# Delta-rule layer: a forward substitution is divided by columns between GpSimd and VectorE, and the query norms move behind GpSimd's share

## The chip, the cores and the metric

The kernel runs on one NeuronCore of a Trainium2 chip. The metric is device time in microseconds (us) of one execution. A core has five engines with a queue each, and each works through its queue in order: TensorE (PE: matmuls and transposes; its weight loads are listed as PEld), VectorE (DVE), ScalarE (ACT), GpSimd (POOL) and SyncE (SP, which here only issues DMAs). Engines wait for each other through semaphores. Before the change the kernel takes 860.06 us (median of 3 runs, 859.24 to 860.62).

## The reference: what is computed

Four residual layers over 256 tokens of width 1024: a pooling mixer, a gated delta-rule layer, an attention layer and the pooling mixer again, all in float32. The change lies in the second, the delta-rule layer. Its core, cut to what matters:

```python
diff = g[..., :, None] - g[..., None, :]
decay = jnp.exp(jnp.where(causal, diff, -jnp.inf))
L = jnp.where(strict, jnp.einsum('bhnid,bhnjd->bhnij', k_beta, k) * decay, 0.0)
A = jnp.eye(C, dtype=L.dtype) + L
sol = lax.linalg.triangular_solve(A, rhs, left_side=True, lower=True)
u_ps, w_cd = sol[..., :dv], sol[..., dv:]
attn = jnp.where(causal, jnp.einsum('bhnid,bhnjd->bhnij', q, k) * decay, 0.0)
...
q = l2norm(q.reshape(B, S, GDN_HEADS, GDN_DK).astype(f32)) * (GDN_DK ** -0.5)
```

There are 8 heads. A unit lower triangular system has to be solved for each head and chunk, and queries and keys are normalised.

## The kernel before

**Precision and weights.** Every large product is three float32r matmuls: a weight tile `raw` is split into `whi` (rounded, ScalarE, L117) and `wlo` (the rest, L119: a subtraction of two tiles in SBUF, on VectorE, or on GpSimd for the k-tiles that the argument `pool` lists). Weights come by SP's queue into three `raw` buffers of two k-tiles each; the split halves sit in rings of nine. So a matmul waits for a `wlo`, a `wlo` for a `whi`, a `whi` for a DMA and for a ring place that a matmul gives back.

**Order.** The program is written in the order of the string `g0 k0 d a0 g1 k1 a1 s q0 v0 i v1 v2 q1 g2 u0 v3 u1 g3` (L559), and a list scheduler (`schedule_with_timeline_sim`, L1242) then sets the order on every engine from its own estimates of time; `tc.issue_after`, wrapped as `later` (L85), holds a step back behind an instruction. That order is fixed when the kernel is built. A projection (`g`, `k`, `q`, `v` and a number) has 8 k-tiles of weights. `k`, `q` and `v` take 96 matmuls of 128x256 each (L127 to L129), then a causal convolution: four ScalarE starts (L633) and 12 VectorE steps (L636), which free the PSUM banks; then a SiLU, and PE transposes (L675 for q and k, L778 for v).

**The substitution.** The chunk here is 128 tokens, so there are 2 x 8 systems of 128x128. Step `a` (L708) writes L transposed to `LT`. Step `s` (L712) inverts the four 32x32 diagonal blocks of each system, 64 blocks in all, one block in a partition: 8 DMAs carry the blocks to DRAM (`d_l`), one brings them back as `Lb` (64 x 32 x 32), and `Tb` starts as 64 unit matrices. Then come 31 rounds r of two GpSimd instructions: an outer product `pr` (L726) of column r of `Lb` below the diagonal and row r of `Tb`, and its subtraction from the rows of `Tb` below r (L730). A round works on 31-r rows and r+1 columns, and each instruction reads what the one before it wrote. `Tb` goes to DRAM (`d_t`, L732) and back in 8 DMAs to the diagonal blocks of `T` (L736). Step `i` (L787) builds the full inverse from `T`: first 16 short matmuls for each of two token tiles (L806) and VectorE's transposes of `T` into `U` (L797), then the rest.

**The query norms.** `queries` (L747) ends with five GpSimd instructions for each half of the heads (L754 to L760): the decay times the queries, and the inverse norm by a power function (`power`, L656). In `values` (L765) GpSimd does the `wlo` of k-tiles 1, 3, 5, 7 of v0 and of 3 and 7 of v1; in `gate` (L551) those of 3 and 7 of g2 and 7 of g3.

Of the kernel before, what the change touches and what calls it, by code (L numbers as in the profile page):

```python
# [13 lines left out]
ALU = mybir.AluOpType  # L14
AX = mybir.AxisListType

P = 128
# [7 lines left out]
EPS = 1e-6  # L25
# [17 lines left out]
def trunk(ctx: ExitStack, tc: tile.TileContext, x, positions, norm_g, pool_w_in, pool_w_grp,  # L43
          pool_scale, pool_w_out, gdn_w_in, gdn_conv, gdn_a_log, gdn_dt_bias, gdn_norm_g,
          gdn_w_out, mla_w_in, mla_q_norm_g, mla_w_uq, mla_kv_norm_g, mla_w_ukv, mla_w_out,
          final_g, out, depth=4, final=True):
    nc = tc.nc
# [22 lines left out]
    def big(name, *dims, dt=F32):  # L70
        return s4.tile([P, *dims], dt, tag="s4", name=name)
# [7 lines left out]
    def small(name, *dims, bufs=2):  # L79
        return sm.tile([P, *dims], F32, tag=name, name=name, bufs=bufs)  # L80
# [4 lines left out]
    def later(*instructions):  # L85

        order = ExitStack()
        for ins in instructions:
            order.enter_context(tc.issue_after(ins))
        return order  # L90


    mark = {}
# [94 lines left out]
    def units(n):  # L188
        return [(k, KU) for k in range(0, n, KU)]
# [141 lines left out]
    def cols_of(w, c0, cols=CW):  # L331
        v = w.rearrange("(k p) c -> p k c", p=P)
        return lambda k0, n: v[:, k0:k0 + n, c0:c0 + cols]
# [201 lines left out]
    def gdn_layer(i, j, hT):  # L535
        H = GDN_H
        M = NT * H
        DV = 256
# [33 lines left out]
        for t in range(NT):  # L572
# [8 lines left out]
                                in1=dtb[:, None, :].to_broadcast([P, NT, H]))  # L581
# [13 lines left out]
                                in1=alog[:, None, :].to_broadcast([P, NT, H]))  # L595
# [14 lines left out]
        for t in range(NT):  # L610
            nc.gpsimd.dma_start(
                out=Gb[t].rearrange("p h s -> p (h s)"),
# [28 lines left out]
        Q, B = 4, 32  # L641
        Tb = big("Tb", B, B)[:M * Q]
# [6 lines left out]
        kT, qT = [], []  # L649
        ktok = big("ktok", H, P)  # L650
        ssq = small("ssq", 2, NT, H, bufs=1)
# [4 lines left out]
        def power(o, a):  # L656
            nc.gpsimd.tensor_tensor(out=o, in0=a, in1=half, op=ALU.pow)
# [25 lines left out]
        def against(dst, rhs, sf, hf, t):  # L683

            ps = bank(aux, "aux").rearrange("p (b s) -> p b s", b=4)
            tt = slice(t * P, (t + 1) * P)
            for b in range(4):
                nc.tensor.matmul(ps[:, b], lhsT=kT[hf][:, b, tt], rhs=rhs[hf][:, b, tt],  # L688
                                 start=True, stop=True)
            for b in range(4):  # L690
                h = 4 * hf + b
                nc.vector.scalar_tensor_tensor(
                    out=dst[t][:, h, :], in0=ps[:, b], scalar=sf[:, t, h:h + 1],
                    in1=DT[t][:, h, :], op0=ALU.mult, op1=ALU.mult)
# [17 lines left out]
        def substitution():  # L712

            d_l = dram.tile([M * Q, B * B], F32, name="d_l")
            lv = d_l.rearrange("(t m d) (r c) -> t d r m c", t=NT, d=Q, r=B)
            for t in range(NT):
                for d in range(Q):
                    nc.sync.dma_start(out=lv[t, d],
                                      in_=LT[t][d * B:(d + 1) * B, :, d * B:(d + 1) * B])
            Lb = big("Lb", B, B)[:M * Q]  # L720
            nc.sync.dma_start(out=Lb, in_=d_l.rearrange("m (r c) -> m r c", r=B))
            pr = small("pr", 256, bufs=1)[:M * Q]
            for r in range(B - 1):
                n, c = B - 1 - r, r + 1
                pv = pr[:, :n * c].rearrange("m (a b) -> m a b", a=n)
                nc.gpsimd.tensor_tensor(out=pv, op=ALU.mult,  # L726
                                        in0=Lb[:, r, r + 1:, None].to_broadcast([M * Q, n, c]),
                                        in1=Tb[:, r:r + 1, :c].to_broadcast([M * Q, n, c]))
                tv = Tb[:, r + 1:, :c]
                nc.gpsimd.tensor_tensor(out=tv, in0=tv, in1=pv, op=ALU.subtract)  # L730
            d_t = dram.tile([M * Q, B * B], F32, name="d_t")
            nc.sync.dma_start(out=d_t.rearrange("m (r c) -> m r c", r=B), in_=Tb)  # L732
            tv = d_t.rearrange("(t m d) (r c) -> t d r m c", t=NT, d=Q, r=B)
            for t in range(NT):
                for d in range(Q):
                    nc.sync.dma_start(out=T[t][d * B:(d + 1) * B, :, d * B:(d + 1) * B],  # L736
                                      in_=tv[t, d])
            nc.vector.reciprocal(rki, rk)
            nc.vector.tensor_tensor(out=kds, in0=rk[:, 0, :], in1=DT[0][:, :, P - 1],
                                    op=ALU.mult)  # L740
            nc.vector.tensor_scalar(neG, eG[:, 1, :], -1.0, None, ALU.mult)
            nc.gpsimd.tensor_tensor(out=ktok, in0=ktok, op=ALU.mult,
                                    in1=kds[:, :, None].to_broadcast([P, H, P]))
# [3 lines left out]
        def queries(hf):  # L747
            if hf == 0:
                at_.extend(big("attnT", H, P) for _ in range(NT))
            channels(qT, 0, hf, 1)  # L750
            for t in range(NT):
                against(at_, qT, rk, hf, t)
            ev = Eb[:, 4 * hf:4 * hf + 4, :]
            nc.gpsimd.tensor_tensor(out=ev, in0=ev, in1=qT[hf][:, :, P:], op=ALU.mult)  # L754
            rh, qh = rq[:, :, 4 * hf:4 * hf + 4], rq2[:, :, 4 * hf:4 * hf + 4]
            nc.gpsimd.tensor_scalar(qh, ssq[:, 1, :, 4 * hf:4 * hf + 4], float(P), EPS * P,
                                    ALU.mult, ALU.add)
            power(rh, qh)
            nc.gpsimd.tensor_tensor(out=qh, in0=rh, in1=rh, op=ALU.mult)
            nc.gpsimd.tensor_scalar(qh, qh, 1.0 / DV, None, ALU.mult)  # L760


        vR = []

        def values(vi):  # L765
            banks = project(cols_of(w_in, 2 * GDN_QK + vi * CW), units(KD), hT, chan=True,
                            pool=((1, 3, 5, 7), (3, 7), (), ())[vi])
            vR.append(big("vR", NT, CW))
            for b in range(2):
                h = 2 * vi + b  # L770
                vc = worka("vc", 2 * S)
                conv(*[(banks[b][:, c * S:(c + 1) * S], 16 + 2 * h + c, vc[:, c * S:(c + 1) * S])
                       for c in range(2)])
                nc.scalar.activation(vc, vc, AF.Silu)
                ps = bank(tps, "tp").rearrange("p (t s) -> p t s", t=NT)
                for t in range(NT):
                    for c in range(2):
                        nc.tensor.transpose(ps[:, t, c * P:(c + 1) * P],  # L778
                                            vc[:, c * S + t * P:c * S + (t + 1) * P], ident)
                for t in range(NT):  # L780
                    nc.scalar.activation(vR[vi][:, t, b * DV:(b + 1) * DV], ps[:, t], AF.Copy,
                                         scale=rki[:, t, h:h + 1])
# [470 lines left out]
```

## Time and profile before

| what | value |
|---|---|
| median of 3 runs | 860.06 us |
| the profiled execution: its time | 859.14 us |
| its span, first to last instruction | 857.4 us |
| around the span (difference) | 1.7 us |
| PE busy | 835.0 us (97%) |
| VectorE, ScalarE, GpSimd busy | 591.2, 488.2, 155.7 us |
| delta-rule layer, roughly | 178 us to 427 us of the span |
| the 31 rounds on GpSimd | 259.8 us to 310.1 us |

In the rows that follow, times are microseconds from the span's start unless marked ns; a timeline row gives start, duration, engine, source line, operation, output and inputs, the shape and how many instructions it merges, and in brackets the engine's idle time before it with what ended that. The table of windows gives the busy time of each engine in a stretch and, as PEclk, the TensorE clock that was granted (1.00 is full).

### The profile page before, as it was taken

How to read it: one execution, taken by the hardware profiler on the slowest of the kernel's cores; microseconds unless marked ns; L12 is line 12 of the kernel's file. 1: busy time of each engine (PE TensorE's matmuls, PEld its weight loads, DVE VectorE, ACT ScalarE, POOL GpSimd, SP SyncE). 2: the span in 40 equal slices, each digit the busy share in tenths (PEclk: the TensorE clock that was granted, in tenths of full speed). 3: DMA queues.
4: the chain of work that ended last, by engine and by line, in shares of the span. 5: the costliest groups of instructions: out<-in, count | busy, mean ns of one | idle time of the engine just before them, and what ended most of it. 6: DMA issues, size and time to landing. Idle time of an engine off the chain costs nothing.

```text
span 857.4 us, 16137 instructions
## 1 busy us (share of the span) xinstructions
PE 835.0 (97%) x5967; PEld 778.7 (91%) x5967; DVE 591.2 (69%) x1138; ACT 488.2 (57%) x1007; POOL 155.7 (18%) x292
## 2 busy tenths in 40 slices
PE   7999999999999969999999999999999999999996
PEld 6999998988999959888979998999989989999986
DVE  4589776456989665656577659778767668866852
ACT  5565555467857435555565654566555476555542
POOL 4000000233248941022212002000000210000012
PEclk9999999999999989999999999999999999999999
DMA  6765556546555462222547676743652547565551
GB/s 199 249 188 188 178 189 213 180 148 206 188 160 176 134 168 102 75 74 99 173 147 215 201 165 172 196 132 95 171 167 79 173 149 218 175 192 183 187 200 50
DMA packets 111288, 140.43 MB, mean 164 GB/s; under 512 B 23340, under 2 KB 53224, under 8 KB 111208
## 3 DMA queue, kind: packets, MB, share of 16 engines
q1 hardware_dynamic: 109056, 138.17, 53.1%
q8 instruction: 47, 0.77, 0.4%
q0 software_dynamic: 320, 1.06, 0.3%
q10 hardware_dynamic: 1832, 0.16, 0.2%
q14 instruction: 33, 0.27, 0.1%
HBM read 137.79 MB, written 1.58 MB: 163 GB/s over the span
## 4 chain that ended last, share of the span: by engine, by line
PE 85%; POOL 7%; DVE 2%; DMA 2%; issue 2%; ACT 1%; SPq 1%; POOLq 0%; ACTq 0%; DVEq 0%
PE acc L167 34%; PE acc L127 12%; PE acc L128 12%; PE acc L129 12%; POOL Tb L730 2%; POOL pr L726 2%; PE aux L127 2%; PE aux L128 2%; PE aux L129 2%; DVE h L303 1%; DMA gain<-in_norm_g_dram 1%; PE aux L688 1%; ACT junk L209 1%; PE aux L806 1%; PE tp L1165 1%
## 5 line engine op out<-in xcount | busy, mean ns | idle before, releaser
L119 DVE TENSOR_TENSOR wlo<-raw,whi 128x512 fp32r<-128x512 f32 (+1 forms) x491 | 338.6, 712 | 163.2 <-ACT whi L117 160.9
L117 ACT CAST whi<-raw 128x512 fp32r<-128x512 f32 (+1 forms) x508 | 301.4, 617 | 261.8 <-PE acc L167 89.8
L127 PE MATMUL acc<-hTh,whi 128*128 128x256 f32 x832 | 235.3, 283 | 1.0 <-DVE cv L636 1.0
L128 PE MATMUL acc<-hTl,whi 128*128 128x256 f32 x832 | 235.8, 283 | 0.0
L129 PE MATMUL acc<-hTh,wlo 128*128 128x256 f32 x832 | 234.7, 282 | 0.0
L127 PEld LDWEIGHTS acc<-hTh,whi 128*128 128x128 f32 x832 | 157.7, 190 | 1.8 <-issue 1.4
L128 PEld LDWEIGHTS acc<-hTl,whi 128*128 128x128 f32 x832 | 157.6, 189 | 0.4
L129 PEld LDWEIGHTS acc<-hTh,wlo 128*128 128x128 f32 x832 | 157.5, 189 | 0.2
L167 PE MATMUL acc<-wlo,yTh 128*128 128x256 f32 (+1 forms) x384 | 116.2, 319 | 0.0
L167 PE MATMUL acc<-whi,yTh 128*128 128x256 f32 (+1 forms) x384 | 116.2, 323 | 0.0
L167 PE MATMUL acc<-whi,yTl 128*128 128x256 f32 (+1 forms) x384 | 92.4, 321 | 0.0
L167 PEld LDWEIGHTS acc<-wlo,yTh 128*128 128x128 f32 x384 | 72.0, 188 | 5.0
L167 PEld LDWEIGHTS acc<-whi,yTh 128*128 128x128 f32 x384 | 71.9, 188 | 5.2
L167 PEld LDWEIGHTS acc<-whi,yTl 128*128 128x128 f32 x384 | 63.1, 188 | 5.6
L291 POOL TENSOR_TENSOR hg<-x,gain 128x256 f32<-128x256 f32 x18 | 14.8, 832 | 259.1 <-DVE x L353 257.4
L167 PE MATMUL acc<-wlo,hTh 128*128 128x512 f32 (+1 forms) x144 | 55.9, 394 | 0.4 <-DVE wlo L119 0.2
L167 PE MATMUL acc<-whi,hTh 128*128 128x512 f32 (+1 forms) x144 | 55.5, 393 | 0.7 <-ACT hTh L195 0.7
L167 PE MATMUL acc<-whi,hTl 128*128 128x512 f32 (+1 forms) x144 | 45.4, 388 | 0.0
L119 POOL TENSOR_TENSOR wlo<-raw,whi 128x512 fp32r<-128x512 f32 x17 | 23.1, 1360 | 70.2 <-ACT whi L117 70.2
L434 POOL COPY win<-u 128x4 f32<-128x4 f32 x8 | 2.8, 354 | 177.0 <-ACT u L428 177.0
L167 PEld LDWEIGHTS acc<-wlo,hTh 128*128 128x128 f32 x144 | 27.3, 190 | 6.8 <-DVE wlo L119 1.7
L167 PEld LDWEIGHTS acc<-whi,hTh 128*128 128x128 f32 x144 | 27.3, 190 | 6.8 <-ACT hTh L195 1.7
(337 smaller groups left out, 1443.3 us busy)
## 6 DMA issues: line engine op xcount, KB each, us to landing
raw<-in_pool_w_in_dram SPq DMA_DIRECT2D x60, 512.0 KB, 4.4
raw<-in_gdn_w_in_dram SPq DMA_DIRECT2D x48, 512.0 KB, 3.9
raw<-in_pool_w_out_dram SPq DMA_DIRECT2D x32, 512.0 KB, 3.7
raw<-in_mla_w_in_dram SPq DMA_DIRECT2D x24, 512.0 KB, 4.4
raw<-in_mla_w_uq_dram SPq DMA_DIRECT2D x36, 256.0 KB, 3.8
raw<-in_pool_w_grp_dram SPq DMA_DIRECT2D x16, 512.0 KB, 4.2
raw<-in_gdn_w_out_dram SPq DMA_DIRECT2D x16, 512.0 KB, 3.5
raw<-in_mla_w_ukv_dram SPq DMA_DIRECT2D x32, 256.0 KB, 3.4
```

What stands on the lines that cost most here:

```text
L117: a = nc.scalar.copy(hi, v)
L119: b = e.tensor_tensor(out=lo, in0=v, in1=hi.bitcast(F32), op=ALU.subtract)
L127: nc.tensor.matmul(o, lhsT=lhs[0], rhs=rhs[0], start=start, stop=False)
L128: nc.tensor.matmul(o, lhsT=lhs[0], rhs=rhs[1], start=False, stop=False)
L129: nc.tensor.matmul(o, lhsT=lhs[1], rhs=rhs[0], start=False, stop=stop)
L167: nc.tensor.matmul(o, lhsT=act(k, t * P, P)[x], rhs=parts[j][z][:, sl], start=k == first and x == z == 0, stop=k == last and x == 1)
L209: nc.scalar.activation(junk[:, :n], src, AF.Square, scale=scale, accum_out=o)
L291: nc.gpsimd.tensor_tensor(out=self.early[t, a], in0=xs[t][:, sl], in1=self.g[:, sl], op=ALU.mult)
L303: nc.vector.scalar_tensor_tensor(out=h[:, cut:], in0=xs[t][:, sl], scalar=r[:, 0:1], in1=self.g[:, sl], op0=ALU.mult, op1=ALU.mult)
L688: nc.tensor.matmul(ps[:, b], lhsT=kT[hf][:, b, tt], rhs=rhs[hf][:, b, tt], start=True, stop=True)
L726: nc.gpsimd.tensor_tensor(out=pv, op=ALU.mult, in0=Lb[:, r, r + 1:, None].to_broadcast([M * Q, n, c]), in1=Tb[:, r:r + 1, :c].to_broadcast ...
L730: nc.gpsimd.tensor_tensor(out=tv, in0=tv, in1=pv, op=ALU.subtract)
```

## The change

The 31 rounds become two independent runs, since a column of the inverse depends on no other column. GpSimd solves columns 0 to 5 in 31 rounds of at most six columns (temporary `prp`). VectorE solves columns 6 to 31 in the 25 rounds from 6 on, which have 31-r rows and r-5 columns (temporary `prv`): 50 instructions. The five query-norm instructions may be issued on GpSimd only after its last subtraction (`mark["blocks"]`), for both halves. And the two `wlo` of v1 that GpSimd did go to VectorE. The program's DMAs are the same in number and size.

```diff
--- before.py
+++ after.py
@@ -719,15 +719,19 @@
                                       in_=LT[t][d * B:(d + 1) * B, :, d * B:(d + 1) * B])
             Lb = big("Lb", B, B)[:M * Q]
             nc.sync.dma_start(out=Lb, in_=d_l.rearrange("m (r c) -> m r c", r=B))
-            pr = small("pr", 256, bufs=1)[:M * Q]
-            for r in range(B - 1):
-                n, c = B - 1 - r, r + 1
-                pv = pr[:, :n * c].rearrange("m (a b) -> m a b", a=n)
-                nc.gpsimd.tensor_tensor(out=pv, op=ALU.mult,
-                                        in0=Lb[:, r, r + 1:, None].to_broadcast([M * Q, n, c]),
-                                        in1=Tb[:, r:r + 1, :c].to_broadcast([M * Q, n, c]))
-                tv = Tb[:, r + 1:, :c]
-                nc.gpsimd.tensor_tensor(out=tv, in0=tv, in1=pv, op=ALU.subtract)
+
+            for e, name, c0, c1 in ((nc.gpsimd, "prp", 0, 6), (nc.vector, "prv", 6, B)):
+                tmp = small(name, 200, bufs=1)[:M * Q]
+                for r in range(c0, B - 1):
+                    n, c = B - 1 - r, min(r + 1, c1) - c0
+                    pv = tmp[:, :n * c].rearrange("m (a b) -> m a b", a=n)
+                    e.tensor_tensor(out=pv, op=ALU.mult,
+                                    in0=Lb[:, r, r + 1:, None].to_broadcast([M * Q, n, c]),
+                                    in1=Tb[:, r:r + 1, c0:c0 + c].to_broadcast([M * Q, n, c]))
+                    tv = Tb[:, r + 1:, c0:c0 + c]
+                    end = e.tensor_tensor(out=tv, in0=tv, in1=pv, op=ALU.subtract)
+                if e is nc.gpsimd:
+                    mark["blocks"] = end.ins
             d_t = dram.tile([M * Q, B * B], F32, name="d_t")
             nc.sync.dma_start(out=d_t.rearrange("m (r c) -> m r c", r=B), in_=Tb)
             tv = d_t.rearrange("(t m d) (r c) -> t d r m c", t=NT, d=Q, r=B)
@@ -751,20 +755,22 @@
             for t in range(NT):
                 against(at_, qT, rk, hf, t)
             ev = Eb[:, 4 * hf:4 * hf + 4, :]
-            nc.gpsimd.tensor_tensor(out=ev, in0=ev, in1=qT[hf][:, :, P:], op=ALU.mult)
             rh, qh = rq[:, :, 4 * hf:4 * hf + 4], rq2[:, :, 4 * hf:4 * hf + 4]
-            nc.gpsimd.tensor_scalar(qh, ssq[:, 1, :, 4 * hf:4 * hf + 4], float(P), EPS * P,
-                                    ALU.mult, ALU.add)
-            power(rh, qh)
-            nc.gpsimd.tensor_tensor(out=qh, in0=rh, in1=rh, op=ALU.mult)
-            nc.gpsimd.tensor_scalar(qh, qh, 1.0 / DV, None, ALU.mult)
+
+            with later(mark["blocks"]):
+                nc.gpsimd.tensor_tensor(out=ev, in0=ev, in1=qT[hf][:, :, P:], op=ALU.mult)
+                nc.gpsimd.tensor_scalar(qh, ssq[:, 1, :, 4 * hf:4 * hf + 4], float(P), EPS * P,
+                                        ALU.mult, ALU.add)
+                power(rh, qh)
+                nc.gpsimd.tensor_tensor(out=qh, in0=rh, in1=rh, op=ALU.mult)
+                nc.gpsimd.tensor_scalar(qh, qh, 1.0 / DV, None, ALU.mult)
 
 
         vR = []
 
         def values(vi):
             banks = project(cols_of(w_in, 2 * GDN_QK + vi * CW), units(KD), hT, chan=True,
-                            pool=((1, 3, 5, 7), (3, 7), (), ())[vi])
+                            pool=((1, 3, 5, 7), (), (), ())[vi])
             vR.append(big("vR", NT, CW))
             for b in range(2):
                 h = 2 * vi + b
```

The scheduler answers with another order on every engine, in the stretch from q0 to u1 above all. Line numbers from L735 on are larger by 4 to 6 in the changed kernel (L732 there is the subtraction, L784 the transpose of v, L812 the first matmul on `T`).

VectorE, where `Lb` has landed. `Tb` and `prv`, `pr` are the substitution's; `attnT` and `ssq` belong to q0, `vc_3467` and `vc_3484` (before), `vc_3518` and `vc_3535` (after) are the two convolved halves of v0. Before:

```order
L119 TENSOR_TENSOR wlo_3822<-raw_3820,whi_3823 128x512
L679 TENSOR_REDUCE ssq_2522<-sq_3294 128x2x2
L692 SCALAR_TENSOR_TENSOR attnT_3124<-aux_3305,rk_2523,DT_2496 128x128 x4
L679 TENSOR_REDUCE ssq_2522<-sq_3302 128x2x2
L692 SCALAR_TENSOR_TENSOR attnT_3125<-aux_3314,rk_2523,DT_2497 128x128 x4
L636 SCALAR_TENSOR_TENSOR vc_3467<-acc_3328,tap_648,vc_3467 128x255
L636 SCALAR_TENSOR_TENSOR vc_3484<-acc_3329,tap_648,vc_3484 128x255
L119 TENSOR_TENSOR wlo_3826<-raw_3820,whi_3827 128x512
```

Now, at the same place:

```order
L119 TENSOR_TENSOR wlo_3839<-raw_3837,whi_3840 128x512
L728 TENSOR_TENSOR prv_3110<-Lb_3045,Tb_2514 64x25
L732 TENSOR_TENSOR Tb_2514<-Tb_2514,prv_3110 64x25
L728 TENSOR_TENSOR prv_3110<-Lb_3045,Tb_2514 64x48
L732 TENSOR_TENSOR Tb_2514<-Tb_2514,prv_3110 64x24x2
L728 TENSOR_TENSOR prv_3110<-Lb_3045,Tb_2514 64x69
L679 TENSOR_REDUCE ssq_2522<-sq_3345 128x2x2
L732 TENSOR_TENSOR Tb_2514<-Tb_2514,prv_3110 64x23x3
L728 TENSOR_TENSOR prv_3110<-Lb_3045,Tb_2514 64x88
L692 SCALAR_TENSOR_TENSOR attnT_3175<-aux_3356,rk_2523,DT_2496 128x128
L732 TENSOR_TENSOR Tb_2514<-Tb_2514,prv_3110 64x22x4
```

The rounds now stand between VectorE's other work, from here to four `wlo` before its transposes of `T`; between the first and the last of them stand 26 `wlo`, all 36 convolution steps of v0, v1 and v2, and 6 of q1.

PE, at the transposes of v0 (`tp`), between matmuls of v2 (`acc_3784`, `acc_3785` before, `acc_3835`, `acc_3836` after). Before:

```order
L129 MATMUL acc_3785<-hTh1_2267,wlo_3856 128x256
L778 MATMUL tp_3477<-ident_101,vc_3467 128x128 x4
L127 MATMUL acc_3785<-hTh1_2267,whi_3857 128x256
L128 MATMUL acc_3785<-hTl1_2268,whi_3857 128x256
L129 MATMUL acc_3785<-hTh1_2267,wlo_3856 128x256
L127 MATMUL acc_3784<-hTh1_2267,whi_3861 128x256
L128 MATMUL acc_3784<-hTl1_2268,whi_3861 128x256
L129 MATMUL acc_3784<-hTh1_2267,wlo_3860 128x256
L127 MATMUL acc_3784<-hTh1_2267,whi_3861 128x256
L128 MATMUL acc_3784<-hTl1_2268,whi_3861 128x256
L129 MATMUL acc_3784<-hTh1_2267,wlo_3860 128x256
L778 MATMUL tp_3494<-ident_101,vc_3484 128x128 x4
```

Now:

```order
L127 MATMUL acc_3835<-hTh0_2258,whi_3878 128x256
L128 MATMUL acc_3835<-hTl0_2259,whi_3878 128x256
L129 MATMUL acc_3835<-hTh0_2258,wlo_3877 128x256
L784 MATMUL tp_3528<-ident_101,vc_3518 128x128 x4
L784 MATMUL tp_3545<-ident_101,vc_3535 128x128 x4
L127 MATMUL acc_3836<-hTh0_2258,whi_3840 128x256
L128 MATMUL acc_3836<-hTl0_2259,whi_3840 128x256
L129 MATMUL acc_3836<-hTh0_2258,wlo_3839 128x256
```

Both groups of transposes stand together now, 95 matmuls behind the products of q0's keys and queries (L688), where the first stood 125 and the second 134 matmuls behind them. From those products to the first matmul on `T` there are 299 matmuls of 128x256 and 48 of 128x512 before, and 302 and 48 now.

## The prediction

> **What bounds the kernel now.** I read the waits of PE over the delta-rule layer first, then the chain of work that ended last, PE's timeline, and the table of windows. PE is busy for 97% of the span, and of its waits in this layer one is long: the first matmul on `T` waits for the DMA that brings `T` back.
>
> ```profile
> PE 835.0 (97%) x5967; PEld 778.7 (91%) x5967; DVE 591.2 (69%) x1138; ACT 488.2 (57%) x1007; POOL 155.7 (18%) x292
> ```
>
> ```profile
> PE aux L806 <- DMA T<-d_t: 7.4, 1, 7.4
> PE acc L127 <- DVE cv L636: 1.0, 1, 1.0
> ```
>
> ```profile
> 310.12 2.94 DMA d_t<-Tb
> 313.98 2.02 DMA T<-d_t
> ```
>
> ```profile
> 259.78 0.23 POOL L726 TENSOR_TENSOR pr<-Lb,Tb 64x31 f32<-64x31 f32 x1 [1.25 <-DMA Lb<-d_l]
> 309.85 0.24 POOL L730 TENSOR_TENSOR Tb<-Tb,pr 64x31 f32<-64x31 f32 x1
> ```
>
> ```profile
> 308.45 0.28 PE L129 MATMUL acc<-hTh,wlo 128*128 128x256 f32 x1
> 316.09 3.65 PE L806 MATMUL aux<-T,LT 128*128 128x64 f32 x16 [7.36 <-DMA T<-d_t]
> 320.07 0.42 PE L129 MATMUL acc<-hTh,wlo 128*128 128x256 f32 x1
> 326.57 1.89 PE L806 MATMUL aux<-T,LT 128*128 128x64 f32 x16
> ```
>
> GpSimd's rounds run from 259.78 to 310.09; 6.0 us later, at 316.09, PE has `T`. It had finished what it had at 308.73 and so idles 7.36 us. Then it runs at half clock:
>
> ```profile
> 265.00:275.00 10.00, 10.00 (x87) 10.00 (x87) 10.00 (x20) 6.54 (x14) 9.45 (x14) 1.00 0.56 161
> 315.00:325.00 10.00, 8.91 (x45) 8.94 (x46) 4.88 (x6) 4.50 (x11) 0.00 (x0) 0.54 0.61 179
> 325.00:335.00 10.00, 10.00 (x99) 9.84 (x99) 6.35 (x12) 6.18 (x14) 1.69 (x2) 1.00 0.20 58
> ```
>
> The sixteen matmuls of L806 take 3.65 us there and 1.89 at full clock (1.8 lost), and the 15 of 128x256 that follow it by 324.6 come 0.21 us apart instead of 0.118 (1.4 lost); with eight slowed transposes (estimate 0.6) the half clock costs 3.8 us. With the 1.0 us wait for `cv` the stretch loses 7.4 + 3.8 + 1.0 = 12 us: that is all that an earlier `T` could save. In the window from 265 to 275 (columns: PE, PEld, DVE, ACT, POOL busy) VectorE is as full as PE: 10.00 of 10.00 us.
>
> **The change part by part.** *GpSimd's share.* A round's instruction has (31-r) rows by at most six columns: 2 x 2,531 = 5,062 elements in 62 instructions, against 10,912 before.
>
> ```profile
> 260.44 0.28 POOL L726 TENSOR_TENSOR pr<-Lb,Tb 64x60 f32<-64x60 f32 x1
> 264.62 0.46 POOL L726 TENSOR_TENSOR pr<-Lb,Tb 64x156 f32<-64x156 f32 x1
> ```
>
> From 0.28 us for 60 elements to 0.46 for 156 is 1.9 ns an element and 0.17 us fixed; with the gap of 0.08 between instructions 62 x 0.25 + 5,062 x 0.0019 = 25 us. The old rounds took 50.3 us, 6.3 of them other instructions in between; by the same formula they would be 36, so some 8 us were contention. GpSimd will end between 285 and 295, long before it is needed. Behind it stand the query norms and the first half's product, now 4 us of GpSimd (1.27 and 1.67 the longest), and then two `wlo` of g2, which PE needs after 300: no cost. The norms held back are first read here:
>
> ```profile
> 366.43 0.20 POOL L900 TENSOR_TENSOR oss<-oss,rq 128x2 f32<-128x2 f32 x1 [21.93 <-ACT junk L209]
> ```
>
> That is 70 us later, and GpSimd idles 22 us before it, so this part costs nothing either.
>
> *VectorE's share* is the term that decides. It has 2 x 2,925 = 5,850 elements in 50 instructions, none of which the trace has on VectorE. The nearest rows:
>
> ```profile
> 196.90 0.17 DVE L589 TENSOR_SCALAR beta<-beta 128x16 f32<-128x16 f32 x1 [0.71 <-ACT beta L585]
> 197.01 0.17 DVE L587 TENSOR_SCALAR e<-e 128x16 f32<-128x16 f32 x1
> 199.26 0.17 DVE L593 TENSOR_SCALAR sp<-sp 128x16 f32<-128x16 f32 x1
> 199.46 0.17 DVE L594 TENSOR_TENSOR lga<-sp,alog 128x16 f32<-128x16 f32 x1
> 244.08 0.15 DVE L703 TENSOR_TENSOR s<-rk,beta 128x8 f32<-128x8 f32 x1
> ```
>
> ```profile
> L119 DVE TENSOR_TENSOR wlo<-raw,whi 128x512 fp32r<-128x512 f32 x11 | 7.2, 687 | 5.5 <-ACT whi L117 5.5
> ```
>
> Independent small instructions start 0.11 us apart, dependent ones (L594 reads what L593 wrote) 0.20: about 0.09 and 0.18 fixed. From 0.15 us at 8 elements to 0.687 at 512 it is 1.07 ns an element. In the changed order 16 of the 50 stand right behind the one that they read: 16 x 0.18 + 34 x 0.09 + 5,850 x 0.00107 = 12.2 us. The rest of what VectorE does from the first of them to the last:
>
> ```profile
> 287.21 2.03 DVE L636 SCALAR_TENSOR_TENSOR vc<-acc,tap,vc 128x254 f32<-128x254 f32 x5
> 355.84 2.16 DVE L692 SCALAR_TENSOR_TENSOR attnT<-aux,rk,DT 128x128 f32<-128x128 f32 x8 [0.41 <-PE aux L688]
> 259.61 0.67 DVE L679 TENSOR_REDUCE ssq<-sq 128x4 f32<-128x512 f32 x1
> ```
>
> 42 convolution steps at 0.39 (16.4), 26 `wlo` at 0.60 start to start (15.6), 8 `attnT` at 0.27 (2.2), two sums at 0.60 (1.2): 35.4 us. Together 47.6 us, so from 259.8 VectorE ends its columns at 307.4 at the earliest. `Lb` may land half a microsecond sooner, as a weight load now stands behind the `d_l` DMAs and not among them on SP's queue; I leave that out. SP's other DMAs keep their places. The wait of the first one for `Lb` holds up q0's sums and `attnT` behind it; the first of these started at 259.61, so by 0.2 us.
>
> *Contention between the two shares* has no row of its own and needs bounds. Below: nothing. Above, these rows:
>
> ```profile
> 244.49 1.90 POOL L742 TENSOR_TENSOR ktok<-ktok,kds 128x1024 f32<-128x1024 f32 x1 [0.89 <-DVE kds L739]
> 245.11 1.30 DVE L705 TENSOR_TENSOR s<-s,rk 128x8 f32<-128x8 f32 x1
> ```
>
> ```profile
> L119 DVE TENSOR_TENSOR wlo<-raw,whi 128x512 fp32r<-128x512 f32 x20 | 16.9, 851 | 0.6 <-ACT whi L117 0.6
> ```
>
> L705 has the form of L703 and takes 1.30 us instead of 0.15: it ends with GpSimd's `ktok`, at 246.4. So an instruction of VectorE with two SBUF inputs can be held until GpSimd's is done. `wlo`, `prv` and the subtraction are all of this kind; the convolution reads PSUM. If VectorE had to stand aside for all of GpSimd's 25.5 us (20 in the rounds without gaps, 5.5 in the four long ones behind them), and 42% of that fell on VectorE's other work (19.8 of 47.6 us), it would lose 0.58 x 25.5 = 15 us. Between the ends I go by the group of 20 `wlo` measured beside the busy rounds, from 259.6 to 292.7: 851 ns against 687, so 0.16 us each. About 15 `wlo` and 30 of the new instructions fall into GpSimd's time: 45 x 0.16 = 7.2, and 1.3 for the long instructions behind: 8.5 us. VectorE ends at 315.9, `T` is there at 321.9.
>
> The Trainium skill (SBUF — State Buffer, section "Who interferes with whom") says that a VectorE instruction with two SBUF inputs and a GpSimd instruction that reads SBUF share a port under an exclusive lock, held for the whole instruction. L705's 1.30 us agrees; the 851 ns of the `wlo`, beside a GpSimd that was busy nearly all the time, show mild blocking. By the rule at its strictest the sum would take the upper bound, which is a rival below.
>
> *PE's order.* Now, 95 matmuls behind q0's products, PE comes to both groups of v0's transposes. At 0.118 us each from 258.96 this is 270.2.
>
> ```profile
> 258.96 0.37 PE L128 MATMUL acc<-hTl,whi 128*128 128x256 f32 x1
> 272.92 0.63 ACT L774 ACTIVATE vc<-vc 128x512 f32<-128x512 f32 x1
> 273.83 0.60 PE L778 MATMUL tp<-ident,vc 128*128 128x128 f32 x4
> ```
>
> Before, the first group came at 273.83, when its SiLU was just ready. Now VectorE must first have done 13 of the new instructions (2.7 us), the sums and `attnT` (3.4), 8 `wlo` (4.8) and 15 convolution steps (5.9): 16.8 us, or 20 with 0.16 for each of 21; from 259.8 that is 279.8, and with the SiLU 280.4. PE, which holds weights enough, stands still from 270.2 for 10 us (at least 6.9), and queued behind it is all the rest of v2, q1 and g2. After so long a wait I count half clock again, 3.8 us. Its remaining work to the first matmul on `T` is 207 matmuls (24.4), 48 of 0.233 (11.2, by the rows below) and 16 transposes (estimate 1.4, from the four in 0.60):
>
> ```profile
> 291.55 0.40 PE L167 MATMUL acc<-whi,hTh 128*128 128x512 f32 x1
> 302.28 0.62 PE L167 MATMUL acc<-whi,hTl 128*128 128x512 f32 x2
> ```
>
> 280.4 + 37.0 + 3.8 = 321.2, as late as `T`. So PE will hardly wait for `T`, but only because it has already waited.
>
> *The sum.* The first matmul on `T` moves from 316.1 to 321.9: +5.8. The half clock behind it goes: -3.8. Three more matmuls precede it, which saves 0.35 behind it. Work after it is alike and PE is full there, so the shift stays: +1.7, in round numbers +2. On the profiled execution, 859.14 (857.4 of span and 1.7 around it), this is about 861; the median lies 0.9 above that run, so **862**. Less than 0.2%, some 1.7 us, a measurement of this kernel cannot tell from no change.
>
> **The rivals.** *Faster: the port costs VectorE nothing.* `T` arrives at 307.4 + 6.0 = 313.4, PE at 277.3 + 37.0 = 314.3, or 318.1 if it ran at half clock after its 6.9 us. Both then at full clock: 314.3 or 318.1 - 316.1 - 3.8 - 0.35, so -6.0 or -2.2, around 856. For it: GpSimd's pieces are shorter than before, at most 0.46 us, and in the old rounds it was GpSimd that waited more. Against it: L705.
>
> *Slower, clearly: the lock is strict.* From the point where GpSimd's reads keep VectorE out whenever they run, VectorE ends at 307.4 + 15 = 322, `T` is there at 328; PE, ready at 321 to 322, idles 6 us and falls to half clock once more. +12: 871 to 872. For it: L705, and all three kinds of instruction need the port. Against it: the 851 ns.
>
> *No change.* VectorE loses 5 us rather than 8.5, or PE's stop costs no clock; the wait moved from `T` to v0's transposes, with the same sum: 859.5 to 861. It needs nothing but a smaller term, and is also what would stand if the change did not shorten GpSimd's run; that it does, the order shows.
>
> **How the numbers follow.** My forecast, slower by 1 to 7 us with VectorE as the bound, has 0.45, its own range being 860 to 867; most of that, 0.38, lies beyond 0.2%. The faster rival has 0.27, the strict lock 0.13, no change 0.15. Faster by over 0.2%: 0.27. Slower by over 0.2%: 0.38 + 0.13 = 0.51. Within: the remaining 0.22. The range must take in the faster rival and half of the strict lock: 855.5 to 869.
>
> **What would show it.** In the changed profile: VectorE's last subtraction at 312 to 319 (307 speaks for the faster rival, 322 for the lock); GpSimd's last at 285 to 296; a PE wait of 7 to 11 us at L784 from about 270, released by ScalarE or VectorE; PE's wait at L812 under 4 us and the granted clock near 1.00 behind it; `wlo` between 260 and 290 at 0.8 to 0.9 us. I am wrong in the mechanism if PE has no wait at L784, and in the main term if the new instructions on VectorE differ much from 12 us in sum, or if VectorE, always full by my count, stands idle waiting for ScalarE or PE among its rounds.

## The result, and the profile after

The changed kernel takes 868.3 us (median of 5 executions, 862.22 to 870.37), the kernel before 859.24 us (5, 858.65 to 860.62): ratio 1.0092, 95% interval 1.0067 to 1.0117, so slower by 8 to 9 us. A second set (6 executions against 17) gave 867.69 us and 1.0099 [1.0081, 1.0116]. The profile shown here is of the shortest execution, 862.22 us with a span of 860.5; a second profile, of an execution of 867.86 us (span 866.1), shows what the typical one adds.

PE's waits in the delta-rule layer, changed kernel (columns: us in total, times, longest):

```profile
PE acc L127 <- DVE vc L636: 8.2, 1, 8.2
...
PE aux L812 <- DMA T<-d_t: 0.9, 1, 0.9
```

The 7.4 us wait for `T` is nearly gone, and a stop of 8.2 us for v0's convolution (`vc`) stands in its place. PE's timeline shows where; then VectorE's first and last round, GpSimd's last, and the way of `T` from the chain of waits:

```profile
276.23 0.55 PE L127 MATMUL acc<-hTh,whi 128*128 128x256 f32 x1 [8.19 <-DVE vc L636]
...
280.85 1.36 PE L784 MATMUL tp<-ident,vc 128*128 128x128 f32 x8
...
319.71 2.00 PE L812 MATMUL aux<-T,LT 128*128 128x64 f32 x16 [0.93 <-DMA T<-d_t]
```

```profile
258.52 0.18 DVE L728 TENSOR_TENSOR prv<-Lb,Tb 64x25 f32<-64x25 f32 x1 [0.19 <-DMA Lb<-d_l]
...
284.96 0.70 DVE L119 TENSOR_TENSOR wlo<-raw,whi 128x512 fp32r<-128x512 f32 x1 [0.89 <-ACT whi L117]
...
290.36 0.69 DVE L119 TENSOR_TENSOR wlo<-raw,whi 128x512 fp32r<-128x512 f32 x1 [0.99 <-ACT whi L117]
...
311.57 0.18 DVE L732 TENSOR_TENSOR Tb<-Tb,prv 64x25 f32<-64x25 f32 x1
```

```profile
294.24 0.26 POOL L732 TENSOR_TENSOR Tb<-Tb,prp 64x6 f32<-64x6 f32 x1
```

```profile
311.77 5.03 DMA d_t<-Tb
...
317.74 1.93 DMA T<-d_t
```

GpSimd is through at 294.5 instead of 310.1, but VectorE only at 311.75, and `T` reaches PE at 319.71, 3.6 us *later* than before. The stopped PE is the first matmul of v2: in the new order v2's first PSUM bank is one of the two that v0 held, and this bank is free when VectorE has done v0's convolution on it. In the kernel before, v2's two banks had served q0's transposes and products, and v0's two went to q1, later. The compiled programs of split_only, no_gp, hold and a_v3 below hand v2 the same bank of v0 as the changed kernel; those that give VectorE no columns do not. The windows (PE, PEld, DVE, ACT, POOL busy, then the granted clock) show VectorE full up to 275 and the lower clock that comes with the stop:

```profile
265.00:275.00 10.00, 3.05 (x26) 2.84 (x25) 10.00 (x22) 3.11 (x7) 9.22 (x11) 0.81 0.58 165
275.00:285.00 10.00, 8.77 (x54) 8.80 (x55) 8.87 (x26) 4.45 (x10) 8.27 (x23) 0.67 0.12 46
...
320.00:330.00 10.00, 10.00 (x92) 9.81 (x92) 6.29 (x9) 5.80 (x14) 0.00 (x0) 1.00 0.26 66
```

Cut at the start of each layer's norm, the delta-rule, attention and last layer read as follows (length, PE busy, clock, DMA). First the kernel before, then the changed one, then its longer execution:

```profile
171.91:427.17 255.26, 246.48 (x1703) 0.98 0.47 143
427.17:686.42 259.25, 258.87 (x1842) 1.00 0.56 158
686.42:857.40 170.98, 163.74 (x1221) 0.99 0.53 170
```

```profile
171.52:428.85 257.33, 245.97 (x1703) 0.98 0.46 142
428.85:690.24 261.39, 260.97 (x1858) 1.00 0.55 157
690.24:860.50 170.26, 162.27 (x1206) 0.99 0.54 171
```

```profile
172.42:434.39 261.97, 248.06 (x1703) 0.97 0.45 139
434.39:695.84 261.45, 261.04 (x1858) 1.00 0.55 157
695.84:866.10 170.26, 162.22 (x1205) 0.99 0.53 171
```

Three parts, then. The two later layers, whose code is the same, together cost 1.4 us more in both profiles (261.39 + 170.26 against 259.25 + 170.98): the scheduler's order changed there too. (The two are read as a sum, since 16 more matmuls lie ahead of the cut between them.) The delta-rule layer costs 2.1 us more in the short execution and 6.7 us in the other. What the longer one adds is seen in these rows of it (PE's waits, VectorE's and PE's timeline, a window):

```profile
PE acc L127 <- DVE vc L636: 8.9, 1, 8.9
```

```profile
260.95 0.18 DVE L728 TENSOR_TENSOR prv<-Lb,Tb 64x25 f32<-64x25 f32 x1 [1.15 <-DMA Lb<-d_l]
...
315.45 0.18 DVE L732 TENSOR_TENSOR Tb<-Tb,prv 64x25 f32<-64x25 f32 x1
```

```profile
323.89 2.00 PE L812 MATMUL aux<-T,LT 128*128 128x64 f32 x16 [2.25 <-DMA T<-d_t]
```

```profile
325.00:335.00 10.00, 10.00 (x80) 10.00 (x80) 5.29 (x8) 5.34 (x13) 0.00 (x0) 0.83 0.23 61
```

Counted from the layer's start, `Lb` comes 1.5 us later (at 88.5 against 87.0 us) and the rounds take 54.7 us against 53.2, and so PE waits for `T` as well, 2.25 us, and then loses clock a second time.

### The profile page after: what moved, and what is told of

It is laid out like the page before. It is cut to its first block, busy times and chain, and to the rows that moved or that the text cites. A ratio compares the mean times of both kernels' runs of the same rounds, so it can differ in the third digit from the quotient of the medians.

```text
span 860.5 us, 16184 instructions
## 1 busy us (share of the span) xinstructions
PE 835.1 (97%) x5967; PEld 776.1 (90%) x5967; DVE 600.8 (70%) x1190; ACT 490.4 (57%) x1007; POOL 144.6 (17%) x290
## 4 chain that ended last, share of the span: by engine, by line
PE 86%; DVE 6%; DMA 3%; POOL 2%; issue 1%; ACT 1%; SPq 0%; POOLq 0%; ACTq 0%
PE acc L167 33%; PE acc L128 13%; PE acc L127 13%; PE acc L129 13%; PE aux L127 2%; PE aux L128 2%; PE aux L129 2%; DVE wlo L119 2%; DMA raw<-in_pool_w_in_dram 1%; PE aux L688 1%; PE tp L1171 1%; DVE vc L636 1%; DMA d_t<-Tb 1%; DVE h L303 1%; DMA Lb<-d_l 1%
## 5 line engine op out<-in xcount | busy, mean ns | idle before, releaser
L167 PE MATMUL acc<-wlo,hTh 128*128 128x512 f32 (+1 forms) x144 | 56.1, 395 | 1.0 <-DVE wlo L119 1.0
L167 PEld LDWEIGHTS acc<-whi,hTl 128*128 128x128 f32 x144 | 26.9, 190 | 6.0 <-DVE hTl L200 0.5
```

What stands on the lines that cost most here:

```text
L167: nc.tensor.matmul(o, lhsT=act(k, t * P, P)[x], rhs=parts[j][z][:, sl], start=k == first and x == z == 0, stop=k == last and x == 1)
```

## The experiments

Theory A: VectorE is full from the arrival of `Lb`, and its own new work sets both v0's convolution and `T`. Theory B: it is contention between the two engines. Theory C: the loss comes from the other parts of the change, or from order elsewhere. All times are medians against the kernel before on the same chip.

| kernel | us | ratio [95%] |
|---|---|---|
| changed, again | 867.69 | 1.0099 [1.0081, 1.0116] |
| split_only | 866.78 | 1.0077 [1.0050, 1.0105] |
| others_only | 860.02 | 1.0007 [0.9996, 1.0018] |
| cut14 | 869.36 | 1.0117 [1.0103, 1.0131] |
| no_gp | 863.29 | 1.0042 [1.0028, 1.0055] |
| hold | 875.36 | 1.0191 [1.0171, 1.0211] |
| halves | 859.36 | 0.9995 [0.9983, 1.0006] |
| b_v3 | 865.67 | 1.0073 [1.0058, 1.0088] |
| a_v3 | 877.64 | 1.0205 [1.0187, 1.0222] |
| hn_mid1 | 859.18 | 0.9998 [0.9984, 1.0011] |
| best_try | 851.33 | 0.9899 [0.9884, 0.9914] |
| queue_before | 863.70 | 1.0043 [1.0030, 1.0057] |

**The changed kernel again.**

> The changed kernel unaltered, timed again beside the kernel before; its five times lay between 862.2 and 870.4 us, and the profile at hand is of the 862.2 one. Theory A (VectorE's order is the bound and it is near its limit everywhere in this stretch): the profile of a slower run shows the extra 4 to 7 us in the delta-rule layer, as a longer PE stop at v2's first matmul or as a wait on T that the fast run lacks, and half clock behind it. Theory C (the loss lies elsewhere, in the order of the attention layer): the delta-rule layer stays at 257 us and the attention layer grows beyond 261 us. If the spread comes from the chip as a whole, all layers grow alike and the median may come out near 862.

The extra lies in the delta-rule layer, as theory A said, and the attention layer repeats to 0.1 us. The 1.4 us of theory C are there too, but constant.

**Which part of the change.** Only the division of the columns, and only the other two parts:

```diff
 split_only: from the changed kernel
-            with later(mark["blocks"]):        # norms in their old place
-                            pool=((1, 3, 5, 7), (), (), ())[vi])
+                            pool=((1, 3, 5, 7), (3, 7), (), ())[vi])
 others_only: from the changed kernel
-            for e, name, c0, c1 in ((nc.gpsimd, "prp", 0, 6), (nc.vector, "prv", 6, B)):
+            for e, name, c0, c1 in ((nc.gpsimd, "prp", 0, B),):
```

> Only the division of the columns: the norms stay among GpSimd's rounds, and GpSimd keeps the two wlo of v1. Theory A: nothing that VectorE does is changed but two wlo (1.3 us), so PE still stops for v0's convolution, 7 to 8 us, and the time is 865 to 869 us. If GpSimd's part or the moved wlo mattered more than the division: 860 or less.

> Only the other two parts: the norms held behind GpSimd's last subtraction and v1's two wlo on VectorE, while GpSimd solves all 32 columns as before. Theory A: GpSimd loses 6.3 us of other instructions among its rounds and ends near 304, T is there near 310, PE waits 1 to 2 us in place of 7.4 and need not fall to half clock: 849 to 853 us. If the loss of the change comes from these two parts or from a new order in the attention layer, this kernel shows it too: 861 us or more.

The division alone carries the loss; its PE stop is 9.5 us. The other two parts cost nothing, but they gain nothing either, against my 849 to 853. From others_only's timeline and waits:

```profile
307.75 0.68 POOL L732 TENSOR_TENSOR Tb<-Tb,prp 64x31 f32<-64x31 f32 x1
```

```profile
PE aux L812 <- DMA T<-d_t: 7.3, 1, 7.3
```

GpSimd ends at 308.4 and not at 304: the rounds took 48.3 us, although only 44.0 of the old 50.3 were their own. `T` is there 1.6 us sooner, at 314.5, and PE came to it 1.6 us sooner as well, at 307.15 instead of 308.73: in this program 2,158 matmuls and transposes of PE stand ahead of the first matmul on `T`, where the kernel before has 2,181. The wait stayed as long as it was. This was the first sign that an earlier `T` is not by itself a gain.

**Fewer columns on VectorE.**

```diff
-            for e, name, c0, c1 in ((nc.gpsimd, "prp", 0, 6), (nc.vector, "prv", 6, B)):
+            for e, name, c0, c1 in ((nc.gpsimd, "prp", 0, 14), (nc.vector, "prv", 14, B)):
```

> The changed kernel with the cut at column 14 in place of 6: VectorE has 34 instructions and 1,938 elements in place of 50 and 5,850, by its rates in the changed profile some 7 us in place of 15, and GpSimd 62 instructions with 8,974 elements, some 33 us without contention. Theory A: v0's convolution ends 4 to 6 us earlier, PE stops 2 to 4 us in place of 8, GpSimd ends near 298 and T comes near 305: 853 to 858 us. Theory B (contention at the port is the cost, in proportion to the time in which both engines work on SBUF): GpSimd works longer, so VectorE's end hardly moves, 862 to 868 us.

Both expectations failed. PE's stop fell to 1.9 us, as A said, but not by the lighter work alone: in this program v0's first bank goes to v2's second, and the stop stands there, 45 matmuls further on. `T` came at 322.93 and PE waited 5.8 us for it, although VectorE had less to do. VectorE's timeline:

```profile
307.98 0.75 DVE L119 TENSOR_TENSOR wlo<-raw,whi 128x512 fp32r<-128x512 f32 x1 [8.05 <-ACT whi L117]
...
315.82 0.17 DVE L732 TENSOR_TENSOR Tb<-Tb,prv 64x17 f32<-64x17 f32 x1
```

In VectorE's order a `wlo` stands ahead of the last four and a half rounds, and its weights come late (ScalarE waits 8.2 us for their DMA to make the `whi`; why it was late is open); VectorE idles 8 us with rounds queued behind. So it is not the amount of VectorE's work alone: the rounds stand in one queue with the weight splits, and `T` came no earlier than the weights ahead of its last round let it.

**Contention by itself.** GpSimd's rounds but the first are left out; VectorE's and PE's orders stay.

```diff
-                for r in range(c0, B - 1):
+                for r in range(c0, B - 1 if c0 else 1):
```

> The changed kernel with GpSimd's 31 rounds cut to the first one; the rest of its share is left out, so the output is not the reference's. The order of VectorE and PE is the changed kernel's row by row. It measures what GpSimd's rounds cost VectorE. In the changed kernel VectorE's rounds took 53.2 and 54.7 us from the first instruction to the last. Contention as I summed it (8.5 us): about 45 us, PE's stop at v2's first matmul 3 to 5 us in place of 8 to 9, T 8 us earlier, 859 to 861 us. VectorE's own work alone (theory A without contention): 52 us or more, and the time stays at 866 to 868 us. The strict lock: 40 us or less.

```profile
260.60 0.18 DVE L728 TENSOR_TENSOR prv<-Lb,Tb 64x25 f32<-64x25 f32 x1 [1.20 <-DMA Lb<-d_l]
...
312.30 0.18 DVE L732 TENSOR_TENSOR Tb<-Tb,prv 64x25 f32<-64x25 f32 x1
```

```profile
PE acc L127 <- DVE vc L636: 8.7, 1, 8.7
```

The rounds take 51.9 us, against 53.2 and 54.7 with GpSimd at work. `Lb` lands as late here as in the longer execution of the changed kernel (88.6 and 88.5 us after the layer's start), so these two compare: GpSimd's rounds cost VectorE 2.8 us, and the strict lock is out. The `wlo` between 258 and 316 have a mean of 680 ns without the rounds and 721 with them. First no_gp, then the changed kernel:

```profile
L119 DVE TENSOR_TENSOR wlo<-raw,whi 128x512 fp32r<-128x512 f32 x30 | 20.2, 680 | 5.6 <-ACT whi L117 5.5
```

```profile
L119 DVE TENSOR_TENSOR wlo<-raw,whi 128x512 fp32r<-128x512 f32 x30 | 21.5, 721 | 5.8 <-ACT whi L117 5.8
```

This is not all of the contention. no_gp keeps the long instructions of GpSimd (the norms, now right behind its one round, and two `wlo` of g2), and they hold three of VectorE's new instructions. In no_gp's timeline these are the three, then the GpSimd instruction beside the last of them:

```profile
261.04 1.55 DVE L728 TENSOR_TENSOR prv<-Lb,Tb 64x48 f32<-64x48 f32 x1
...
298.63 1.02 DVE L728 TENSOR_TENSOR prv<-Lb,Tb 64x144 f32<-64x144 f32 x1
...
304.07 1.25 DVE L728 TENSOR_TENSOR prv<-Lb,Tb 64x120 f32<-64x120 f32 x1
```

```profile
303.30 1.89 POOL L119 TENSOR_TENSOR wlo<-raw,whi 128x512 fp32r<-128x512 f32 x1 [3.81 <-ACT whi L117]
```

Undisturbed, instructions of these three forms take 0.23, 0.29 and 0.27 us in these traces, so 3.0 us are lost here. That is why the fifty new instructions are busy as long without GpSimd's rounds (16.4 us) as with them (16.5). For contention as a whole I set each of VectorE's 128 instructions of the stretch against the shortest of its form: 5.0 us are lost in the short execution of the changed kernel, 5.5 in the longer one, 3.8 in no_gp (an estimate, since not every excess need be contention). PE's stop is no shorter in no_gp, but 1.3 of its 8.7 us are the first of the three holds, which stands ahead of v0's convolution.

The time, 863.3 (862.6 to 863.9), is 4.4 us below the changed kernel of the other set, and none of the times that were expected. 2.8 us at VectorE's end became more, since `T` without them is just covered (a wait of 0.84 us), and with them is not (2.25 us and the clock behind it). So about half of the loss goes with GpSimd's rounds. The other 3.8 us are VectorE's own work, the new order and what the long instructions still hold; with those holds gone too, some 861 us would be left (estimate: 1.3 us less of the stop, no wait for `T`), which is no gain.

**The rounds held behind v0's convolution.**

```diff
+        def columns():                      # new step "w", written behind v0
+            with later(mark["conv"]):       # v0's last convolution step
+                rounds(nc.vector, "prv", 6, B, Lb_[0])
```

> The changed kernel with VectorE's rounds held behind v0's convolution, the same instructions otherwise. Theory A (VectorE is full from the arrival of Lb to its last round, so T's time is set by the sum of its work): PE no longer stops at v2's first matmul, but VectorE ends its rounds no earlier than 310, T lands at 317 to 321, PE waits there 8 to 12 us instead, and the time is 864 to 870 us. If PE's stop at v2 was the loss by itself: 858 to 861 us.

```profile
PE aux L821 <- DMA T<-d_t: 6.5, 1, 6.5
PE acc L127 <- DVE vc L636: 5.2, 1, 5.2
```

As A said, the wait moves to `T`, but worse than I put it: `T` at 326.2, 875 us. And PE still stops 5.2 us at v2's first matmul, although the first round starts only at 275.4, behind v0's convolution. So of the 8 to 9 us the rounds make 3 to 4; the rest comes with the new order, which hands v2 a bank of v0 here too, and A does not explain that.

**Is it the order that brings PE to `T` too early?** Step `i` written behind v3, before the change and after it:

```diff
-        order = "g0 k0 d a0 g1 k1 a1 s q0 v0 i v1 v2 q1 g2 u0 v3 u1 g3".split()
+        order = "g0 k0 d a0 g1 k1 a1 s q0 v0 v1 v2 q1 g2 v3 i u0 u1 g3".split()
```

> The kernel before with one edit in the order string: step i (the first matmuls on T) is written behind v3, and so PE comes to them 8.4 us of its work later (71 matmuls of 128x256); the substitution is untouched. If the loss at T is that the written-out order brings PE to T too early (theory E), the wait of 7.4 us and the 3.8 us of half clock go, and nothing else grows: 849 to 853 us. If PE needs v3's matmuls behind T, as cover for the chain of short steps that follows, they are missed there and it waits again in other places: 856 to 860 us or more.

> The same edit of the order string in the changed kernel. Its wait for T is short already (0.8 to 2.3 us); the stop of 8 to 9 us at v2's first matmul stays, since VectorE has the same work ahead of v0's convolution. Theory A (VectorE's rounds are the cost): at most the 2.3 us and a part of the half clock behind T are saved, 861 to 867 us, some 10 us above the kernel before with the same edit. If the changed kernel only suffered from its order: near that one.

In b_v3 the wait for `T` is gone, and yet 6 us are lost: PE waits 3.0 us for q1 and, behind `T`, the clock falls in the chain of short steps that v3 used to cover:

```profile
PE tp L675 <- ACT kqT L669: 3.0, 1, 3.0
```

```profile
340.00:350.00 10.00, 7.89 (x49) 7.24 (x48) 2.57 (x5) 0.58 (x1) 0.00 (x0) 0.62 0.16 52
350.00:360.00 10.00, 8.32 (x56) 7.78 (x56) 1.54 (x3) 0.58 (x1) 0.00 (x0) 0.50 0.00 0
```

My 849 to 853 was wrong; the rival that I had named held. In a_v3 the stop for v0's convolution stayed (8.3 us), and the changed kernel remains 12 us above its counterpart, as A said; the 861 to 867 that A put on it were missed by 10 us.

**A substitution that leaves VectorE alone.** GpSimd solves even columns on partitions 0 to 63 and odd ones on 64 to 127, with 2,856 elements for each kind of instruction in place of 5,456; hn_mid1 and best_try add to it.

```diff
 halves: from the kernel before
-                n, c = B - 1 - r, r + 1
+                n, c = B - 1 - r, r // 2 + 1      # Lb, Tb and pr on 128 partitions
-                                    T[t].rearrange("p m c -> p (m c)"))
+                                    T[t].rearrange("p m (d x j) -> p (m d) j x", d=Q, x=2))
 hn_mid1: halves, and
+            with later(mark["blocks"]):           # the norms, as in the change
-                            pool=((0, 4), (7,), (3, 7), (7,))[vi])
+                            pool=((0, 4), (7,), (), (7,))[vi])
+                    if k == mid[0]: mid[1]()      # step i, behind k-tile 1 of v3
 best_try: hn_mid1 with k-tile 3, the norms behind the T transfers, and
-                nc.sync.dma_start(out=d_t.rearrange("m (r x j) -> x m r j", r=B, x=2)[x],
+                nc.gpsimd.dma_start(out=d_t.rearrange("m (r x j) -> x m r j", r=B, x=2)[x],
-                    nc.sync.dma_start(out=T[t][d * B:(d + 1) * B, :, d * B:(d + 1) * B],
+                    nc.gpsimd.dma_start(out=T[t][d * B:(d + 1) * B, :, d * B:(d + 1) * B],
+                (nc.sync, nc.gpsimd)[x].dma_start(out=Lb[x * M * Q:(x + 1) * M * Q],
```

> A version meant to beat both, made from the kernel before: GpSimd alone solves all columns, but the even ones on partitions 0 to 63 and the odd ones on 64 to 127, with half the columns in each instruction (2,976 elements in 31 instructions of each kind at most, against 5,456). Lb is loaded twice, Tb written by two DMAs, and the columns are put back in order where T is read. By 0.25 us an instruction and 1.9 ns an element, with the old norms and 6 us of contention: 62 x 0.25 + 5,700 x 0.0019 + 6 + 6 = 38 us, end near 298, T near 305, before PE comes to it at 308. If the wait for T and the half clock behind it are the whole loss that can be saved, 849 to 852 us. If PE only waits elsewhere (a wlo, v0's transposes, a reordered stage): 855 to 860 us.

> A version meant to beat both: GpSimd solves even and odd columns on two halves of its partitions (as in halves), the norms are held behind its last subtraction (as in the change), g2's two wlo go from GpSimd to VectorE, which stood idle there, and step i is written behind the second k-tile of v3, so that PE comes to T where the kernel before does. GpSimd should end near 295 and T land near 303, PE comes to it near 308. Theory E: no wait for T, no wait for g2's wlo, full clock: 847 to 851 us. If the chain behind T lacks cover, 853 to 857 us.

> hn_mid1 with four edits more: d_t and T are moved by GpSimd's own DMA queue, so that no weight transfer stands behind them in SP's queue (in hn_mid1 SP issued nothing from 285.6 to 301.1, the DMA share fell to 0.01, and PE waited 8.0 us for q1); the second load of Lb goes by the same queue; the norms stand behind the T transfers; and step i is written behind the fourth k-tile of v3, 2.8 us of PE's work later. If SP's blocked queue is what put the wait back into hn_mid1: PE waits under 3 us in 300 to 320, 848 to 853 us. If the time that T saves is used up by the chain of short steps behind it in any order: 856 to 860 us.

> The kernel before with d_t and the eight T transfers issued by GpSimd's queue in place of SP's, nothing else. GpSimd's rounds and T's arrival stay where they are or come a little later (310 and 316 to 319). If SP's blocked queue matters in the kernel before too (VectorE waited 6.38 us there for a whi at 299.62), weights come sooner, more work stands ahead of T in PE's order, the wait for T shrinks to 3 to 5 us, and the time is 853 to 857 us. If only the length of the rounds counts (theory A's view of the kernel before): 859 to 862 us.

In halves GpSimd ends at 300.5 and PE has `T` at 308.60, 7.5 us earlier than before, for a gain of nothing (0.9995):

```profile
308.60 3.64 PE L814 MATMUL aux<-T,LT 128*128 128x64 f32 x16 [5.72 <-DMA T<-d_t]
```

The scheduler had placed `T`'s matmul earlier too, behind 2,132 matmuls and transposes in place of 2,181, so PE came to it at 302.9 and waited 5.7 us again, with half clock behind. In hn_mid1 `T`'s place is close to the old one (2,190) and no wait for `T` is left, but the time, 859.18, missed both expectations. SP's queue shows the next bound, and the window what it does to the transfers (the last two columns are DMA share and GB/s); then PE's longest wait:

```profile
265.31 20.30 SPq L104 DMA_DIRECT2D raw<-in_gdn_w_in_dram  x8
301.06 0.57 SPq L741 DMA_DIRECT2D d_t<-Tb  x1
```

```profile
290.00:300.00 10.00, 10.00 (x60) 8.72 (x60) 3.44 (x7) 2.21 (x5) 8.35 (x22) 1.00 0.01 2
```

```profile
PE tp L680 <- ACT kqT L674: 9.0, 2, 8.0
```

`d_t` waits for `Tb` at the head of SP's queue for 15 us, and no weight moves meanwhile: PE starves at q1. In best_try SP's queue, that window, that wait, and VectorE's and PE's first work on `T` read

```profile
264.76 54.37 SPq L104 DMA_DIRECT2D raw<-in_gdn_w_in_dram  x16
```

```profile
290.00:300.00 10.00, 10.00 (x60) 8.61 (x58) 3.22 (x6) 2.40 (x6) 8.06 (x23) 1.00 0.39 121
```

```profile
PE tp L680 <- ACT kqT L674: 2.1, 1, 2.1
```

```profile
314.50 2.45 DVE L809 STREAM_TRANSPOSE U<-T 128x1024 f32<-128x1024 f32 x2 [1.62 <-DMA T<-d_t]
...
316.80 1.90 PE L818 MATMUL aux<-T,LT 128*128 128x64 f32 x16
```

and it is 1.0% faster than the kernel before, at 851.33 us. PE comes to `T` at 316.80 and does not wait, although `T` is there only some 2 us earlier than before (314.5 by VectorE's transposes of it). Its four edits over hn_mid1 were not run apart. queue_before shows that the queue alone is no gain: there `d_t` took 4.71 us, `T` came at 319.70, 9.4 us behind GpSimd's last round in place of 6.0, PE waited 6.8 us for it, and the time rose by 0.4%, beyond both expectations.

## Why the prediction was right or wrong

The forecast (862, range 855.5 to 869, slower 0.51) had the right side and the right bound, but its middle was 6 us too low. 868.3 and 867.69 also lie above the 860 to 867 that the mechanism itself was given; the range holds them only because its upper end was drawn for half of the strict lock, which did not come. That part is luck. And two of the signs of being wrong that the prediction named did show: PE has no wait at L784, and VectorE stands idle among its rounds, waiting for ScalarE's `whi` (1.9 us in the short execution, 2.6 in the longer one).

- **GpSimd's share, the norms, the moved `wlo`:** right. The end was predicted at 285 to 295 and came at 294.5 (298.1 in the longer execution); others_only shows that the small parts cost nothing. GpSimd's own rounds took 35.9 us where 25 were worked out without contention, so the conflict of the two engines fell mostly on GpSimd, which had the time.
- **VectorE ends its columns at 315.9:** 311.75, or 53.2 us after its first round in place of 56.1, from terms that erred both ways. Contention was put at 8.5 us and is about 5 by the estimate above: for the rounds I had 7.2, and they cost 2.8 at most; for the long instructions I had 1.3, and they cost about 2 (two instructions of VectorE, a `wlo` of 1.55 us and a `prv` of 1.26). `wlo` came at 721 ns, not at 800 to 900. The rest was put at 47.6: no_gp's 51.9 less 3.0 of holds and 1.6 of waits for `whi` is 47.3, so its sum was right, but the waits were missing, since I had counted VectorE as always full.
- **The rivals:** the strict lock is refuted at VectorE (about 5 us, not 15). The free port was not run as such: without GpSimd's rounds it is still 1.0042 [1.0028, 1.0055], and the estimate without the other holds is no gain either.
- **PE stops 10 us (at least 6.9) at v0's transposes, from 270.2:** 8.19 us from 268.04, released by the same convolution, but 21 matmuls earlier, at v2's first matmul. The step that failed is that I looked only for readers of `vc`, not for the next owner of its PSUM bank. That the size came near is partly luck: the convolution was done at 276.1, not at 279.8, and hold shows that more than half of the stop is there without rounds ahead of the convolution.
- **Half clock, 3.8 us moved from `T` to the stop:** the 21 matmuls from 276.23 to 280.85 took 4.6 us instead of 2.5, and the transposes 0.2 more: 2.4 us in all, less than I took.
- **`T` is 6.0 us behind the last round:** 8.0. `d_t` took 5.03 us instead of 2.94. The DMA engines were 87% busy during it (294 GB/s) where they had been 62% busy (118 GB/s), so more weight transfers beside it are the likely cause; no run isolates it.
- **Under 4 us of wait and full clock at `T`:** 0.93 us and 1.00 in the short execution. The sum of the layer, +1.7, came out at +2.1, but by errors that cancel, which is luck: counted from the layer's start, the first matmul on `T` moved by 4.0 us and not by 5.8, and behind it 1.9 us were won and not 4.15. One of those errors is a sign. The three more matmuls ahead of `T` are counted from q0's products, which themselves stand six places earlier; so three more follow `T` (345 of 128x256 up to the layer's end against 342) and cost the 0.35 us that the sum took off. In the longer execution the two terms are +7.3 and -0.6.
- **"Work after it is alike, so the shift stays":** wrong by 1.4 us in the two later layers. Every kernel with the cut at column 6 shows 1.4 to 1.8 us there and cut14 3.3; those without a share for VectorE stay within 0.3 us of the kernel before.
- **The median 0.9 above the profiled run:** this is where the 6 us went. Stop and `T` were predicted to balance (PE at 321.2, `T` at 321.9), and they do: so 1 to 3 us more on VectorE's chain, which the other execution has, are paid in full, with the clock on top. I counted the balance as cover and should have counted it as an edge.

What stays open: why the scheduler hands v2 a bank of v0 once VectorE has columns to solve; what the stop would be with another bank, which no run tried; and which edit of best_try is worth how much.

## What to carry to other kernels

When an order is fixed by a scheduler's estimates, an earlier result moves its reader forward too, and the wait may stay: before speeding up a producer, see what PE would do in the meantime, and whether its weights can arrive. Work given to an in-order engine delays all that stands behind it and is itself delayed by what stands ahead (a `wlo` that waits for weights, a DMA that waits at the head of SP's queue); and a PSUM bank's next owner waits for the last reader (8.2 us here) just as a reader of the data does. Where two waits come out even, price the case in which either is late.

## What the runs showed of the hardware

- GpSimd's 62 short instructions beside VectorE's own cost VectorE 2.8 us in 54.7, far less than I took from one row (L705, 1.30 us), while GpSimd's rounds took 35.9 us for the 25 that I had worked out. Single instructions do wait for each other whole: VectorE's of 1.25 us above ended with GpSimd's `wlo` beside it, and GpSimd's subtraction below takes 3.27 us, where its product of 156 elements took 0.46 us in the kernel before. The Trainium skill (SBUF — State Buffer, "Who interferes with whom") calls the port that the two engines share an exclusive lock. These rows agree with that; the sum on VectorE stayed small all the same.

```profile
264.50 3.27 POOL L732 TENSOR_TENSOR Tb<-Tb,prp 64x150 f32<-64x150 f32 x1
```

- A wait of 0.93 us left PE's clock at 1.00; one of 2.25 us was followed by 0.83 in the ten microseconds from 325.
- The same 256 KB of `d_t` took 2.94 us in the kernel before, with the DMA engines 62% busy, and 5.03 in the changed one, with 87% (5.46 in its longer execution).
